# Modulation from float32 blocks, sums of weights on GpSimd, and a joined pair of tiles in the last product

## The chip, the cores and the metric

One core of a Trainium2 chip runs the whole kernel. The metric is the device time of one execution in microseconds (us). The engines are TensorE (PE, with its weight loads listed as PEld), VectorE (DVE), ScalarE (ACT), GpSimd (POOL) and SyncE (SP), which issues the DMA transfers.

## What is computed

Two layers act on 256 context tokens and 1024 latent tokens of width 1024; the last layer gives latent tokens only. A layer is:

```python
mod  = (silu(c)    @ ada_w + ada_b)      # 6 x 1024 values for latent tokens
modc = (silu(c_ctx) @ ada_w + ada_b)     # the same for context tokens
y  = mixer(x * (1 + sc1) + sh1, ...)     # input projection, two attentions, chunk gating, output projection
x  = layer_norm(ALPHA * x + g1 * y)
u  = dwconv3((x * (1 + sc2) + sh2) @ ffn_wup)
gate, val = split(u)
x  = layer_norm(ALPHA * x + g2 * ((silu(gate) * val) @ ffn_wdown))
```

`ada_w` is 1024 x 6144 per layer and meets only two vectors, `silu(c)` and `silu(c_ctx)`. `ffn_wup` is 1024 x 5632 and `ffn_wdown` 2816 x 1024.

## The kernel before, in words

**Precision.** Large products run in float32r on pairs: an operand is split into `hi` (a cast, mostly ACT, line 460) and `lo` (the rest, a subtraction on DVE or POOL, line 457), and a product is three matmuls (`mm3`, line 449). Small products use float32 directly; the trace shows two weight loads and two matmuls for each float32 matmul of the program.

**Order.** `Sched` (line 129) places every task by a table of assumed durations. A task has a key, which is its number in the program plus an offset; the lowest key that is ready goes first. `MODKEY` (120) is the offset of the modulation pieces and of the sums. The result is a fixed instruction stream per engine; SP issues its DMAs in that order, and a DMA that must wait holds those behind it.

**Modulation.** `mod_piece` (line 683) makes 256 of the 6144 values: 1 MB of `ada_w` is loaded in two or four blocks and split into `hi` and `lo`; 16 matmuls have the 4 columns of `s4` (the two vectors, high and low) as weights and 256 columns of `ada_w` moving; ACT copies the 4 x 256 result out, and two float32 matmuls with `sel4` add high and low and turn it into columns. There are 48 pieces. Eight are made at the start in `first_hT` (line 778), between the first products of the projection. The other 40 are fillers of `attention` (line 1302): 24 in layer 0, 16 in layer 1.

**Stages.** `first_hT`, then `in_proj` (line 842: chunks z, dk, dv, dq, kv, q, each over up to 10 tiles of 128 tokens), `attention`, `out_tiles`, `ffn` (line 1784). In the trace layer 0 has them at 0 to 85, 85 to 290, 290 to 850, 850 to 1085 (output projection and the first blocks of the up projection), and the rest of the feed-forward part up to 1910 us; layer 1 has its projection at 1910 to 2060, attention to 2570, output projection and first blocks to 2790, and the rest to the end.

**Feed-forward part.** Both products use seven half-size products in place of eight, which need sums of quarter blocks of the weights. For the up projection (22 blocks `f`) `up_load` (line 1554) loads the four quarters of a block and `up_operand` (line 1570) adds them to S1 to S4 (line 1480) before the split. For the down projection the four sums lie in `db` in DRAM. `sums` (line 581) makes them during attention by DMAs of POOL's queue: a copy and an accumulating copy, 16 per layer, 1408 KB each. `down_src` (line 1712) reads them.

**The tail.** The last of the seven down products of layer 1 (`tail` in `ffn`) runs its four pairs of tiles one after another, each over the 11 blocks `p` of weights: 33 matmuls of 512 columns per pair. The operands of `p` are split just before. After each tile's product come its residual sum and its normalisation.

Of the kernel before, what the change touches and what calls it, by code (L numbers as in the profile page):

```python
# [10 lines left out]
F32 = mybir.dt.float32  # L11
F32R = mybir.dt.float32r
# [57 lines left out]
SUMROWS = 704  # L70
# [320 lines left out]
class Kern:  # L391
# [185 lines left out]
    def flat(self, x, c):  # L577

        return x.rearrange("n p c -> (n p) c")[c * SUMROWS:(c + 1) * SUMROWS]

    def sums(self, l):

        x = self.db[l]
        w = lambda a, b: (lambda: self.i["w_down"][l, a, b])
        out = []

        def make(n, c, a, b, r=()):
            key = ("db", l, n, c)
            put = lambda: self.flat(x[n], c)
            kw = dict(w=[key], key=MODKEY, late=40.0)  # L590
            out.append(lambda: self.s.add({"pool": 1.0}, lambda e: self.nc.gpsimd.dma_start(out=put(), in_=self.flat(a(), c), max_dma_last_dim=2048), (), **kw))
            out.append(lambda: self.s.add({"pool": 1.0}, lambda e: self.nc.gpsimd.dma_start(out=put(), in_=self.flat(b(), c), accum_op=ALU.add, max_dma_last_dim=2048), [*r, key], **kw))

        for c in range(NP * P // SUMROWS):
            at = lambda n: ("db", l, n, c)
            make(0, c, w(0, 0), w(0, 1))
            make(1, c, w(0, 1), w(1, 1))
            make(2, c, w(1, 1), lambda: x[0], [at(0)])
            make(3, c, w(1, 0), lambda: x[2], [at(2)])
        return out  # L600

    def begin_sums(self, n):

        for f in self.due[:n]:
            f()
        del self.due[:n]

    def sum_chunks(self, name, l, n, f):
        a, b = f * P * 512, (f + 1) * P * 512 - 1
        m = SUMROWS * 512  # L610
        return [(name, l, n, c) for c in range(a // m, b // m + 1)]
# [28 lines left out]
    def setup(self):  # L640
# [9 lines left out]
        self.s4 = c.tile([P, KD, 4], F32R, tag="s4", name="s4")  # L650
        self.task(act_t(16), lambda e: nc.scalar.activation(s, cc, AF.Silu), ["cT"], ["silu"])
        self.task(dve_t(16), lambda e: nc.vector.tensor_copy(self.s4[:, :, 0:2], s), ["silu"], ["s4a"])
# [1361 lines left out]
```

## Time and profile before

| what | value |
|---|---|
| median of 3 runs | 3407.99 us (3407.11 to 3412.31) |
| the profiled execution | 3411.25 us |
| its span, first to last instruction | 3409.5 us |
| PE busy | 3186.5 us (93%) |
| DVE busy | 2700.5 us (79%) |
| ACT busy | 1677.3 us (49%) |
| POOL busy | 1028.0 us (30%) |
| mean granted clock of PE | 0.967 |
| DMA | 395.40 MB, mean 116 GB/s |

The busy time of an engine is the union of its instructions' times. The granted clock is a share of 2.4 GHz; it is either 1 or 0.5 (1.2 GHz) in any one stretch. In a line of instruction groups, the first number behind the bar is the busy time of the group, the second the mean duration of one instruction (ns). Matmuls overlap, so the distance between two of them is shorter than the duration of one.

### The profile page before, as it was taken

Reading aid. Unit: us, or ns where it says so; the run is one execution under the profiler, and the core shown is the slowest. Engines: PE = TensorE matmul, PEld = TensorE weight load, DVE = VectorE, ACT = ScalarE, POOL = GpSimd, SP = SyncE. Lnnn points to the kernel's source line nnn. Section 1 sums busy time; section 2 is a strip of 40 time slices with the busy share of each in tenths; the row PEclk is TensorE's granted clock in tenths of the full one; section 3 lists DMA queues with packets and bytes.
Section 4 is the critical chain, followed back from the end, with each engine's and each line's share of the span. In section 5 each row is a group of like instructions: output and inputs, shape, how many; then the busy total and the mean of one; then the engine's idle time right before and its main releaser. Section 6 shows DMA issues by size and latency. Waiting matters only on the chain. (4 is left out here: it accounts for less than half of the span.)

```text
span 3409.5 us, 53373 instructions
## 1 busy us (share of the span) xinstructions
PE 3186.5 (93%) x18953; PEld 2785.7 (82%) x18953; DVE 2700.5 (79%) x6407; ACT 1677.3 (49%) x2944; POOL 1028.0 (30%) x631
## 2 busy tenths in 40 slices
PE   7999898998988999999999999989999889999997
PEld 5998887887987888887877898878889867877775
DVE  7567887999768787886687757988998788888687
ACT  5125665666244444544444325665662455545542
POOL 3002554543112111121133302554532232322143
PEclk9999998999999999999999999999999999999998
DMA  6214443442312223225663314353423122323672
GB/s 242 72 52 112 118 124 99 126 108 86 121 69 70 89 72 101 87 86 180 210 204 130 116 58 123 92 135 87 119 88 127 62 80 96 107 98 105 229 258 99
DMA packets 258548, 395.40 MB, mean 116 GB/s; under 512 B 63976, under 2 KB 115688, under 8 KB 258280
## 3 DMA queue, kind: packets, MB, share of 16 engines
q1 hardware_dynamic: 240872, 345.84, 31.4%
q0 software_dynamic: 17408, 46.14, 5.9%
q8 instruction: 149, 2.44, 0.3%
q14 instruction: 119, 0.97, 0.1%
HBM read 311.61 MB, written 126.42 MB: 128 GB/s over the span
## 5 line engine op out<-in xcount | busy, mean ns | idle before, releaser
L447 PE MATMUL t<-region 128*128 128x512 f32 (+4 forms) x15631 | 2853.0, 341 | 137.8 <-DVE region L457 55.0
L447 PEld LDWEIGHTS t<-region 128*128 128x128 f32 x15631 | 2442.1, 192 | 480.0 <-DVE region L457 69.2
L457 DVE TENSOR_TENSOR region<-region 128x512 fp32r<-128x512 f32 (+6 forms) x873 | 760.0, 893 | 176.2 <-ACT region L460 122.7
L460 ACT ACTIVATE region<-region 128x512 fp32r<-128x512 f32 (+4 forms) x944 | 593.9, 663 | 382.8 <-PE t L447 132.5
L460 ACT ACTIVATE region<-t 128x512 fp32r<-128x512 f32 (+4 forms) x948 | 462.1, 514 | 600.0 <-PE t L447 386.3
L457 POOL TENSOR_TENSOR region<-region 128x512 fp32r<-128x512 f32 (+7 forms) x283 | 392.3, 1398 | 1109.3 <-ACT region L460 714.8
L1480 POOL TENSOR_TENSOR region<-region 128x512 f32<-128x512 f32 (+3 forms) x132 | 248.6, 1889 | 823.6 <-DVE region L1667 518.5
L1188 ACT ACTIVATE region<-region,q 128x1280 f32<-128x1280 f32 (+1 forms) x216 | 273.5, 1267 | 175.7 <-DVE q L1187 169.7
L1183 DVE TENSOR_SCALAR_CACHE_REDUCE region<-t 128x512 f32<-128x512 f32 (+1 forms) x600 | 333.7, 584 | 21.3 <-PE t L447 19.1
L457 DVE TENSOR_TENSOR region<-t,region 128x512 fp32r<-128x512 f32 (+1 forms) x529 | 296.9, 595 | 52.8 <-ACT region L460 50.9
L1667 DVE SCALAR_TENSOR_TENSOR region<-region,conv 128x1023 f32<-128x1023 f32 x176 | 231.6, 1325 | 36.7 <-ACT region L1665 36.5
L1480 DVE TENSOR_TENSOR region<-region 128x512 f32<-128x512 f32 (+3 forms) x301 | 226.3, 770 | 2.5 <-DMA da<-region 1.4
L1252 PE MATMUL t<-ident,region 128*128 128x128 f32 x1312 | 184.8, 285 | 24.2 <-DVE region L1225 8.1
L1228 POOL TENSOR_TENSOR region<-region 128x1280 f32<-128x1280 f32 (+1 forms) x68 | 186.8, 2746 | 5.7
L1665 ACT ACTIVATE region<-region,conv 128x1024 f32<-128x1024 f32 x88 | 109.2, 1241 | 159.5 <-DVE region L1648 148.3
L1252 PEld LDWEIGHTS t<-ident,region 128*128 128x128 f32 x1312 | 154.9, 147 | 31.8 <-DVE region L1183 11.0
L1227 POOL TENSOR_SCALAR region<-region,q 128x1280 f32<-128x1280 f32 (+1 forms) x68 | 84.5, 1242 | 210.6 <-DVE q L1222 137.7
L447 PE MATMUL t<-region,s 128*4 128x256 f32 x768 | 119.1, 291 | 17.0 <-DVE region L457 9.2
L447 PEld LDWEIGHTS t<-region,s 128*4 128x4 f32 x768 | 64.6, 87 | 47.4 <-DVE region L457 12.5
L548 POOL TENSOR_TENSOR region<-region 128x1024 f32<-128x1024 f32 x26 | 73.7, 2847 | 95.9 <-DMA region<-n 67.7
L1008 DVE TENSOR_TENSOR region<-t,region 128x256 f32<-128x256 f32 x32 | 13.6, 424 | 107.4 <-PE t L447 107.4
L548 DVE TENSOR_TENSOR region<-region 128x1024 f32<-128x1024 f32 x34 | 62.3, 1841 | 18.2 <-DMA region<-n 17.7
(134 smaller groups left out, 1803.5 us busy)
## 6 DMA issues: line engine op xcount, KB each, us to landing
region<-in_wup SPq DMA_DIRECT2D x176, 256.0 KB, 3.0
region<-in_ada_w SPq DMA_DIRECT2D x160, 256.0 KB, 3.1
da<-region SPq DMA_DIRECT2D x154, 256.0 KB, 3.0
region<-da SPq DMA_DIRECT2D x154, 256.0 KB, 4.1
db<-in_w_down POOLq DMA_DIRECT2D x24, 1408.0 KB, 7.5
region<-db SPq DMA_DIRECT2D x88, 256.0 KB, 4.1
region<-in_w_down SPq DMA_DIRECT2D x66, 256.0 KB, 3.9
n<-region SPq DMA_DIRECT2D x26, 512.0 KB, 3.0
```

The lines of the kernel that those rows point to most:

```text
L447: self.nc.tensor.matmul(ps, a, b, start=start, stop=stop, skip_group_check=again)
L457: eng.tensor_tensor(out=out, in0=full, in1=hi.bitcast(F32), op=ALU.subtract)
L460: self.nc.scalar.activation(out, in_, AF.Copy, **kw)
L548: self.task(engs or pool_t(D), lambda e, row=row, op=op: self.vec[e].tensor_tensor(out=x[:, :D], in0=x[:, :D], in1=row.t, op=op), [x, row] ...
L1183: self.task(dve_t(b - a), lambda e: nc.vector.tensor_scalar(p[:, a:b], ps[:, :b - a], -scale, None, op0=ALU.mult, op1=ALU.min, accum_out=n ...
L1188: self.task(act_t(nk, 0.19), lambda e: nc.scalar.activation(p[:, :nk], p[:, :nk], AF.Exp, bias=m.t, scale=-1.0, accum_out=s.t), [p, m], [p ...
L1227: nc.gpsimd.tensor_scalar(p2[:, :nk], p2[:, :nk], cc.t, 0.0, op0=ALU.mult, op1=ALU.add)
L1228: nc.gpsimd.tensor_tensor(out=p1[:, :nk], in0=p1[:, :nk], in1=p2[:, :nk], op=ALU.add)
L1252: nc.tensor.transpose(ps[:, u, j * P:(j + 1) * P], B[key][j][:, (kt + u) * P:(kt + u + 1) * P], self.ident)
L1480: self.task(engs or either(n), lambda e: self.vec[e].tensor_tensor(out=o(), in0=a(), in1=b(), op=op), r, w, **kw)
L1665: self.task(act_t(n, 0.15), lambda e: nc.scalar.activation(t.t, u(0, n), AF.Identity, scale=c[:, 1:2], bias=c[:, 3:4]), r + ["conv"], [t])
L1667: self.task(dve_t(n - 1, extra=0.06), lambda e, d=d: nc.vector.scalar_tensor_tensor(t[:, 1 - d:n - d], u(d, n - 1 + d), c[:, 2 * d:2 * d + ...
```

## The change

1. `mod_piece` has no split, no `s4` and no `sel4`. The raw float32 block is the weight operand (128 x 128 at a time) and the two columns of `silu` move: 2 halves x 8 steps, 16 float32 matmuls of 2 columns per piece, which write the values as columns at once.
2. The sums of `w_down` are made in `in_proj`: per block `p` SP loads the four quarters (4 x 256 KB), POOL makes four additions of 128 x 512, SP stores four results to `db`. The same is done for the first six blocks of `wup` into a new DRAM tensor `ws`. 17 such groups per layer are hung on the tiles of all chunks but z. POOL's DMAs are gone. For blocks 0 to 5 the up projection loads S1 to S4 ready-made (7 or 8 loads per block in place of 4) and adds nothing.
3. In the tail the first two pairs of tiles share one pass over `p`.

```diff
+    def sums(self, name, l, m):
+        up = name == "ws"
+        out = (self.ws if up else self.db)[l]
+        src = self.i["wup" if up else "w_down"]
+        z = [self.L(F32, (P, 2, HALF)) for _ in range(2)]
...
+                self.dma(lambda j=j, h=h: z[j][:, h], lambda j=j, h=h: src[l, j, h, m], 4 * P * HALF, w=[(z[j], h)], key=MODKEY)
...
+        t = [self.M() for _ in range(4)]
...
+            self.task(pool_t(HALF), lambda e, n=n, a=a, b=b: self.vec[e].tensor_tensor(out=t[n].t, in0=q[a][0](), in1=q[b][0](), op=ALU.add), [q[a][1], q[b][1]], [t[n]], key=MODKEY)
+            self.dma(lambda n=n: out[n, m], lambda n=n: t[n].t, 4 * P * HALF, [t[n]], [(name, l, n, m)], key=MODKEY)
 def mod_piece(self, l, n, key=0, raws=None):
-            w = [self.weight(x, 512, self.M, k=2, key=key, acq=True) for x in src]
...
-                    self.mm(ps[:4, :256], a, hi, h + k == 0, False)
-                    self.mm(ps[:4, :256], a, lo, False, kk * h + k == KD - 1)
-            self.task(mm_t(2 * kk, 256), go, ["s4"] + w[h][1], [ps], key=key, acq=[m4] if h == 0 else ())
-        self.task(act_t(256), lambda e: self.copy(m4[:4], ps[:4, :256]), [ps], [m4], key=key)
...
+            raws = [self.load(self.mod_src(l, n, h)[:, a:a + 512], 512, self.M, key) for h in range(2) for a in (0, 512)]
+            for c in range(2):
+                for k in range(KD):
+                    o = k % kk * 256 + c * P
+                    self.mm(pm[:, c], raws[k // kk][:, o:o + P], self.silu[:, k], k == 0, k == KD - 1)
+        self.task({"pe": 1.8}, go, ["silu", *raws], [pm], key=key)
 def in_chunk(self, l, name, tabs):
-        for t in tiles:
+        for n, t in enumerate(tiles):
+            if name != "z" and n % 4 == 1 and self.pairs_due:
+                self.sums("db", l, self.pairs_due.pop(0))
+            if name != "z" and n % 4 == 3 and self.blocks_due:
+                self.sums("ws", l, self.blocks_due.pop(0))
 def up_operand(self, l, m):
-        if n[0] == "S":
+        if n[0] == "S" and f >= UP_MADE:
 def ffn(self, l):
-                if tail:
+                if tail and m != 1:
                     for p in range(NP):
-                        self.down_mm(banks[t], *held[p], col(t), p, first)
+                        for x, _ in pairs[:2] if m == 0 else [(t, u)]:
+                            self.down_mm(banks[x], *held[p], col(x), p, first)
```

The scratch for dynamic DMAs goes from 2048 to 1024, since POOL issues none now. How the instruction streams move is seen at three places. A row is a run of like instructions of one engine: line, operation, output and inputs, shape, count. Counts of PE are the program's matmuls; a float32 one is two on the chip.

PE at the very start, before. `s` and `sel` are the tables named above, and `region` is any buffer.

```order
L447 MATMUL t<-region,s_70 4x256 x24
L447 MATMUL t<-sel_71,region 128x2 x2
L447 MATMUL t<-region,s_70 4x256 x16
L447 MATMUL t<-sel_71,region 128x2 x2
L447 MATMUL t<-region,s_70 4x256 x16
L447 MATMUL t<-sel_71,region 128x2 x2
L447 MATMUL t<-region,s_70 4x256 x8
L447 MATMUL t<-sel_71,region 128x2 x2
L447 MATMUL t<-region 128x512 x36
```

PE at the very start, now:

```order
L447 MATMUL t<-silu,region 128x2 x64
L447 MATMUL t<-region 128x512 x36
L447 MATMUL t<-silu,region 128x2 x48
L447 MATMUL t<-region 128x512 x36
L447 MATMUL t<-silu,region 128x2 x16
L447 MATMUL t<-region 128x512 x96
```

Four pieces still stand ahead of the first projection products, but in one run, then three, then one.

PE where attention of layer 0 begins, before (line 1168 is a transpose of queries, line 985 one of the projection):

```order
L1168 MATMUL t<-identr,region 128x128 x12
L447 MATMUL t<-region,s_70 4x256 x20
L447 MATMUL t<-sel_71,region 128x2 x2
L985 MATMUL t<-ident,region 128x128 x6
L447 MATMUL t<-region,s_70 4x256 x16
L447 MATMUL t<-sel_71,region 128x2 x2
L447 MATMUL t<-region 128x512 x12
```

The same place now:

```order
L1142 MATMUL t<-identr,region 128x128 x8
L447 MATMUL t<-silu,region 128x2 x48
L959 MATMUL t<-ident,region 128x128 x6
L447 MATMUL t<-region 128x512 x12
L447 MATMUL t<-region 128x256 x24
L447 MATMUL t<-region,sumj 128x256
```

Three pieces stand together here. Of the other 21 of this layer each stands alone; in layer 1 the first two stand together and 14 alone.

POOL in the input projection of layer 0, before, from its last splits of weights on:

```order
L457 TENSOR_TENSOR region<-region 128x1280
L1017 TENSOR_TENSOR region<-region 128x256
L457 TENSOR_TENSOR region<-region 128x1152
L591 DMA db<-in_w_down 704x512
L457 TENSOR_TENSOR region<-region 128x2x2x32
```

POOL there now (line 591 is the addition of a sum):

```order
L591 TENSOR_TENSOR region<-region 128x512 x2
L903 TENSOR_TENSOR region<-region 128x256 x2
L591 TENSOR_TENSOR region<-region 128x512 x16
L457 TENSOR_TENSOR region<-region 128x768
L591 TENSOR_TENSOR region<-region 128x512 x44
L457 TENSOR_TENSOR region<-region 128x1152
L591 TENSOR_TENSOR region<-region 128x512 x3
```

The additions fill POOL's stream there, and on SP their loads and stores stand between the loads of the chunks' weights, the last of which (`w_in_q`) comes behind most of the stores.

## Rows read from the trace of the kernel before

**Rows 1.** The page, busy time of the engines over the span.

```profile
PE 3186.5 (93%) x18953; PEld 2785.7 (82%) x18953; DVE 2700.5 (79%) x6407; ACT 1677.3 (49%) x2944; POOL 1028.0 (30%) x631
```

**Rows 2.** Span and mean granted clock of the core.

```profile
core 0: 3409.5 us, clock 0.967
```

**Rows 3.** Busy time by stage; stretch, length, engines' busy us, clock, DMA share, GB/s.

```profile
0.00:85.00 85.00, 64.79 (x328) 48.07 (x328) 65.08 (x118) 50.27 (x67) 27.36 (x18) 0.94 0.69 243
85.00:290.00 205.00, 203.49 (x1449) 198.24 (x1449) 118.58 (x585) 49.71 (x128) 17.68 (x16) 0.97 0.27 79
290.00:850.00 560.00, 509.32 (x3554) 453.95 (x3554) 481.17 (x1441) 349.90 (x690) 261.58 (x173) 0.95 0.39 108
1085.00:1910.00 825.00, 806.10 (x3991) 677.18 (x3990) 640.69 (x995) 396.31 (x626) 188.08 (x114) 0.99 0.41 130
1910.00:2060.00 150.00, 149.87 (x1120) 147.50 (x1119) 84.29 (x395) 31.07 (x80) 16.86 (x14) 1.00 0.21 66
2060.00:2570.00 510.00, 471.40 (x3283) 421.19 (x3281) 456.35 (x1347) 315.99 (x599) 225.53 (x141) 0.97 0.41 110
2570.00:2790.00 220.00, 194.11 (x1275) 176.61 (x1276) 180.69 (x415) 90.64 (x140) 66.25 (x38) 0.94 0.26 86
```

**Rows 4.** Groups of PE by shape, 35.6 to 38.4 us: modulation's matmuls of 256 columns.

```profile
L447 PE MATMUL t<-region,s 128*4 128x256 f32 x24 | 2.9, 276 | 0.0
```

**Rows 5.** Timeline of PE, 38 to 39.5 us: float32 matmuls of two columns.

```profile
38.43 0.60 PE L447 MATMUL t<-sel,region 4*128 4x2 f32 x4
```

**Rows 6.** Groups of PE by shape, 98.3 to 99.95 us: float32, 64 columns, full clock.

```profile
L447 PE MATMUL t<-region 128*128 128x64 f32 x16 | 1.9, 271 | 0.0
```

**Rows 7.** Groups of PE by shape, 85.3 to 88.3 us: the same at half clock.

```profile
L447 PE MATMUL t<-region 128*128 128x64 f32 x15 | 3.4, 423 | 7.5 <-issue 7.5
```

**Rows 8.** Busy time of three short stretches, columns as in rows 3.

```profile
85.30:88.30 3.00, 3.00 (x15) 3.00 (x15) 3.00 (x20) 0.00 (x0) 0.00 (x0) 0.50 0.00 0
286.30:289.70 3.40, 2.30 (x17) 1.52 (x14) 1.91 (x9) 2.56 (x8) 0.00 (x0) 1.00 0.99 299
289.70:293.10 3.40, 2.90 (x15) 1.57 (x15) 3.34 (x7) 1.96 (x4) 0.00 (x0) 0.50 0.73 256
```

**Rows 9.** Groups by shape, attention of layer 0 (290 to 850 us): splits of 512-column blocks.

```profile
L457 POOL TENSOR_TENSOR region<-region 128x512 fp32r<-128x512 f32 x62 | 82.7, 1345 | 142.1 <-ACT region L460 127.5 <-PE t L1252 7.4 <-DVE q L1220 5.2
L460 ACT ACTIVATE region<-region 128x512 fp32r<-128x512 f32 x94 | 56.6, 628 | 0.2
L457 DVE TENSOR_TENSOR region<-region 128x512 fp32r<-128x512 f32 x32 | 28.6, 901 | 0.4 <-ACT region L460 0.3
```

**Rows 10.** The same in attention of layer 1 (2060 to 2570 us).

```profile
L457 POOL TENSOR_TENSOR region<-region 128x512 fp32r<-128x512 f32 x39 | 52.1, 1343 | 80.4 <-ACT region L460 80.4
L460 ACT ACTIVATE region<-region 128x512 fp32r<-128x512 f32 x66 | 39.6, 627 | 2.4 <-DMA region<-in_ada_w 2.2
L457 DVE TENSOR_TENSOR region<-region 128x512 fp32r<-128x512 f32 x26 | 34.7, 1337 | 0.0
```

**Rows 11.** Groups by shape, whole span: float32 sums of 128 x 512.

```profile
L1480 DVE TENSOR_TENSOR region<-region 128x512 f32<-128x512 f32 x246 | 208.0, 848 | 1.8 <-DMA da<-region 1.4
L1480 POOL TENSOR_TENSOR region<-region 128x512 f32<-128x512 f32 x77 | 125.4, 1631 | 181.6 <-ACT region L1505 78.5 <-issue 25.5 <-DVE region L1764 19.2
```

**Rows 12.** Busy time, 28 to 33 us, columns as in rows 3.

```profile
28.00:33.00 5.00, 5.00 (x19) 3.97 (x18) 3.92 (x5) 2.06 (x2) 0.00 (x0) 0.77 1.02 405
```

**Rows 13.** Timeline of the tail, 3296 to 3410 us; start, length, engine, in brackets idle before.

```profile
3342.42 21.42 POOL L548 TENSOR_TENSOR region<-region 128x1024 f32<-128x1024 f32 x8 [4.23 <-ACT region L544]
3346.36 18.03 DVE L457 TENSOR_TENSOR region<-region 128x512 fp32r<-128x512 f32 x7 [4.68 <-ACT region L460]
3364.44 5.35 PE L447 MATMUL t<-region 128*128 128x512 f32 x14 [1.97 <-DVE region L457]
3372.29 23.34 PE L447 MATMUL t<-region 128*128 128x512 f32 x95 [2.50 <-DVE region L457]
```

More of the change, by code (lines that the diff above doesn't have):

```diff
@@ L69 @@
 UNIT = 64
-SUMROWS = 704
+UP_MADE = 6
 SLACK = 150
@@ L574, in row_from_col @@
         return row
[L577 to L600, printed above, removed]
@@ L649, in setup @@
         s = c.tile([P, KD, 2], F32, tag="silu", name="silu")
[L650 removed]
+        self.silu = s
         self.task(act_t(16), lambda e: nc.scalar.activation(s, cc, AF.Silu), ["cT"], ["silu"])
[L652 to L654 removed]
         self.modv, self.lnv, self.adab, self.inw = [], [], [], {}
@@ L676, in setup @@
         self.dc = d.tile([7, P, NP, P], F32, tag="dc", name="dc")
+        self.ws = [d.tile([4, UP_MADE, P, HALF], F32, tag=f"ws{l}", name="ws") for l in range(DEPTH)]
         self.db = [d.tile([4, NP, P, HALF], F32, tag=f"db{l}", name="db") for l in range(DEPTH)]
@@ L686, in mod_piece, with go @@
         j, q = QUADS[n // 4], n % 4
[L687 to L709 removed]
+        if not raws:
+            raws = [self.load(self.mod_src(l, n, h)[:, a:a + 512], 512, self.M, key) for h in range(2) for a in (0, 512)]
+        kk = KD // len(raws)
+        pm = self.bank(F32, (P, 2, 2))
+        def go(e):
+            for c in range(2):
[3 more added lines that the diff above has]
+        self.task({"pe": 1.8}, go, ["silu", *raws], [pm], key=key)
         ks = slice(2 * q, 2 * q + 2)
@@ L843, in in_proj @@
         tabs = self.tabs if l == 0 else self.z_tables(l)
+        self.pairs_due, self.blocks_due = list(range(NP)), list(range(UP_MADE))
         for name in ZCH:
@@ L1558, in up_load @@
             self.up_loaded += 1
-            for g, h in {"11": [(0, 0)], "12": [(0, 1)], "S1": [(1, 0), (1, 1)]}.get(n, ()):
+            if f < UP_MADE:
+                todo = [n]
+            else:
+                todo = {"S1": ["21", "22"]}.get(n, [n] if n in ("11", "12") else [])
+            for x in todo:
+                if x[0] == "S":
+                    j = int(x[1]) - 1
+                    src, r = self.ws[l][j, f], [("ws", l, j, f)]
+                else:
+                    src, r = self.i["wup"][l, int(x[0]) - 1, int(x[1]) - 1, f], []
                 raw = self.S(F32, (P, HALF))
-                self.dma(lambda raw=raw: raw.t, lambda f=f, g=g, h=h: self.i["wup"][l, g, h, f], 4 * P * HALF, (), [raw])
-                self.up_raw[f, g, h] = raw
+                self.dma(lambda raw=raw: raw.t, lambda src=src: src, 4 * P * HALF, r, [raw])
+                self.up_raw[f, x] = raw
     def up_operands(self, l, m):
@@ L1902, in program @@
             ada = [lambda a=a: self.mod_piece(*a, MODKEY) for a in ada]
-            self.due = self.sums(l)
-            m, d = len(ada), len(self.due)
-            fill = []
-            for j, a in enumerate(ada):
-                fill += [lambda: self.begin_sums(1)] * ((j + 1) * d // m - j * d // m) + [a]
-            self.attention(l, fill)
+            self.attention(l, ada)
             self.out_tiles(l, NT, True)
@@ L1997, in _arrays @@
     a["sel64"] = np.tile(np.eye(64, dtype=np.float32), (2, 1))
-    a["sel4"] = np.tile(np.eye(2, dtype=np.float32), (2, 1))
     return {k: np.ascontiguousarray(v) for k, v in a.items()}
```

41 lines of the change are left out of this document (11 added, 30 removed).

## The prediction

> **What bounds the kernel now.** I read the busy times over the span first. PE is busy 93% of it and DVE 79% [rows 1], so PE is the engine to price; its mean granted clock of 0.967 [rows 2] says that (1 - 0.967) x 2 x 3409.5 = 225 us ran at half clock, which cost some 112 us. Next come the busy times by stage [rows 3]. The input projections (85 to 290 and 1910 to 2060 us) and the long up and down products (1085 to 1910) leave PE idle for 1.5, 0.1 and 19 us: what is taken from DVE there gains little. The attentions are different: PE idles 560.0 - 509.3 = 51 us in layer 0 and 510.0 - 471.4 = 39 us in layer 1, while DVE is busy 86% and 89%. The starts of the up products are like them (layer 1: 2570 to 2790, PE idle 26 us, DVE busy 82%). So a change that moves work from DVE to PE must be read in attention, where 90 us of idle can be won and each us added to PE beyond that is lost.
>
> **The sum's base.** Durations are those of the profiled execution: 3411.25 us, of which 3409.5 are span and 1.75 lie around it. It stands 3.3 us above the median of the runs, 3407.99.
>
> **Modulation, PE's own work.** Before, a piece was 16 matmuls of 256 columns, which follow each other at (2.9 - 0.28)/23 = 0.114 us [rows 4], and four of the float32 matmuls with two columns, at (0.60 - 0.25)/3 = 0.117 us with a duration of 0.25 us [rows 5]: 1.82 + 0.47 = 2.3 us. Now it is 32 float32 matmuls on the chip, each with a 128 x 128 weight load and two columns. No row has this shape exactly. The bounds are two: the two-column matmuls with a weight of 128 columns but 4 rows, 0.117 us [rows 5], and those with a full 128 x 128 weight but 64 columns, (1.9 - 0.27)/15 = 0.109 us [rows 6]. Both say that the moving columns do not set the pace, since 2 and 64 cost the same; the weight load does. I take 0.112: 32 x 0.112 = 3.6 us at full clock. At half clock the 64-column ones follow at (3.4 - 0.42)/14 = 0.213 us [rows 7], so a piece takes 32 x 0.213 = 6.8 us. The 40 pieces in attention thus cost PE 40 x (3.6 - 2.3) = **+52 us** (bounds 48 and 58, by the two prices).
>
> **Modulation, the clock.** From 85.3 to 88.3 us PE was busy 3.00 of 3.00 us with float32 matmuls of 64 columns and their weight loads, and the granted clock was 0.50 throughout [rows 8]; unbroken work of that sort did not bring the clock up. And it fell after a stretch in which PE was busy 2.30 of 3.40 us (286.3 to 289.7) and then stayed at 0.50 for the next 3.4 us [rows 8], which costs 1.7 us of work. A piece has 2 columns per load where those had 64, and nothing else runs on PE while it lasts. I take it that three of four of the 35 pieces that stand alone lose 1.7 us each: 35 x 0.75 x 1.7 = 45. Three pieces together in layer 0 are 96 matmuls; I let a third of them run before the fall and 64 at 0.1 us more each, and 1.7 us is lost behind them: 8. Of the 64 of two pieces in layer 1 I let half run before it: 5. Together **+58 us**, with 0 and 130 (every one twice) as ends. The Trainium skill (TensorE: Matmul & The Clock Gate, section Why this matters for your kernels) asks only that no idle gaps stand between matmul bursts on PE; a piece leaves none, so by that rule this term would be 0 and the forecast 58 us lower. The row at 85.3 us differs from it: busy throughout, at half clock. Whether a weight load counts, the page does not say.
>
> **Modulation, what is relieved.** In attention the subtractions of the split blocks go: DVE loses 28.6 + 34.7 = 63 us, POOL 82.7 + 52.1 = 135 us and ACT 56.6 + 39.6 = 96 us (a few of them belong to other weights) [rows 9, 10]. DVE falls from 938 to 875 of 1070 us. PE's 90 us of idle come from several engines being late by little, and with PE slower too they shrink further: I take **-55 us**, between 0 (the idle lies in chains that do not change) and -80. POOL's DMAs leave as well; I cost that at nothing, DMA being busy 39% and 41% there [rows 3].
>
> **Modulation, the start.** The first 33 us are set by DMA (405 GB/s and a full share of 1.02 [rows 12]), and PE had only 64.8 of 85 us busy [rows 3]. PE starts cold. Now four pieces in a row run at half clock, 4 x 6.8 = 27; then three, a third of them at full clock, 3.6 + 13.6 = 17; then one, 4 to 5: 49 us against 8 x 2.3 = 18. That is +30, +3 for two more returns from half clock, less what of 20 us of idle can take it up: 6.5 at the very start cannot, some 6 between pieces can, and of the 7.5 us that PE waits at 85 us [rows 7] DVE's relief may win 4. With the half clock that the old first pieces had (2.5): **+20 us**, ends +5 and +35.
>
> **Sums on POOL in the projection.** 17 groups of four additions per layer at 1.63 us [rows 11] are 111 us of POOL, which was busy 18 of 205 and 17 of 150 us there [rows 3]: it fits, hidden behind PE. They bring 17 x 2 MB = 36 MB, or 174 and 238 GB/s on top of 79 and 66 [rows 3]; 405 was reached [rows 12]. SP's stores wait for POOL, and behind them wait the chunk weights; these are loaded two blocks ahead (IN_AHEAD), and a chunk lasts about 205/5 = 41 us. If that cover went, the last chunk, q, would start late. **+4 us**, ends 0 and +30. DVE gets slower beside a busy POOL, but has 86 us to spare of 205.
>
> **Ready-made S1 to S4.** 4 x 6 additions per layer leave DVE at 0.85 us [rows 11], 20 us each. Only those near the start of the up product, where PE idles, matter (12 in layer 1 and 8 in layer 0, 17 us of DVE). The extra loads (up to 4 x 256 KB per block) are hidden: 130 GB/s are moved there [rows 3] and 405 can be [rows 12]. **-8 us**, ends 0 and -20.
>
> **The tail.** POOL's 21.4 us of additions hold DVE's subtractions to 18.0/7 = 2.6 us each, and PE is starved from 3353 to 3372 us; then 95 matmuls remain [rows 13]. With two pairs per pass the second pair's 33 matmuls (33 x 23.34/95 = 8 us [rows 13]) fit into that starved time, except those of the last blocks. **-5 us**, ends 0 and -8. The end of the kernel is the last tile's normalisation, which moves with PE.
>
> **Sum.** 52 + 58 - 55 + 20 + 4 - 8 - 5 = +66: 3477 us against the profiled execution, **3474 us** against the median.
>
> **Rivals.** *The clock holds.* If weight loads keep the full clock, the 58 go, and so do about 15 of the start (its seven later records at half clock); the rest is -7, 3401 us. For it: PE is busy without gaps in a piece, all that the rule above asks. Against it: 85.3 us [rows 8]. Range 3385 to 3425.
> *DVE was the bound in attention.* Then the 63 us of DVE and the 135 of POOL decide, not PE: attention loses most of its 90 us of idle and, with fewer stalls, part of the 56 us that it had at half clock in layer 0 and 31 in layer 1 (5% and 3% short of full clock, doubled [rows 3]). That is -80 for the idle and -25 for the clock, against +52, and with the clock's loss around pieces at a quarter of mine (15): -38 instead of +55 in attention; the sum is -27, **3381 us**, faster. It decides from the point where DVE's relief exceeds what PE gains in work, 52 + 15 us. For it: DVE at 89%. Against: PE is busier, at 91 to 92%, and stays.
> *The projection stalls.* POOL's additions, slowed by DVE's work as DVE is by POOL's in the tail [rows 13], take 2.6 us each: 68 x 2.6 = 177 us, longer than layer 1's whole projection (150). SP's stores wait, the weights behind them come late, and PE idles by the difference, 27 us, there and as much in layer 0, where the last weights stand behind most of the stores: 3474 - 4 + 54 = 3524 us.
> That the change fails to relieve DVE is excluded: the splits are gone from the instruction stream.
>
> **Numbers.** The forecast gets 0.60, the clock that holds 0.14, DVE as the bound 0.14, the stall 0.12. 0.2% is about 7 us, what a measurement of this kernel can tell from no change. The forecast's own range, with attention's and the start's ends combined, is 3425 to 3520, and nearly all of it is slower. Of the clock case a third is faster, a third the same, a third slower; the DVE case is faster, the stall slower. Faster 0.17, same 0.06, slower 0.77. The range from 3390 to 3540 leaves out the lower part of the DVE case and the ends of the others.
>
> **What would show it.** In the new profile: two-column matmuls some 0.11 us apart at clock 1 and 0.21 at 0.5; the mean granted clock of both attentions below 0.95 and 0.97, with falls right behind pieces; PE busy more and DVE less there; both attentions longer; the first 85 us stage ending near 105; POOL at about 110 us of the projections and PE still full there; fewer idle us in the tail. The forecast is wrong if the clock stays up through the pieces, or if PE's idle time in attention falls by more than PE's work grows.

## The result and the profile after

The changed kernel takes **3521.37 us** in the median of 4 runs (3499.86 to 3527.49). The kernel before, timed beside it, takes 3409.84 us (3407.11 to 3412.31). The ratio is 1.0316, with a 95% interval of 1.027 to 1.0362: slower. The forecast was 3474 us, in a range of 3390 to 3540. The profiled execution took 3517.12 us.

The page's busy times, which answer to [rows 1], and the core's span and clock, which answer to [rows 2]:

```profile
PE 3312.9 (94%) x19529; PEld 2955.8 (84%) x19529; DVE 2647.9 (75%) x6279; ACT 1567.0 (45%) x2726; POOL 1037.9 (30%) x632
```

```profile
core 0: 3515.3 us, clock 0.948
```

PE is busy 126 us longer, while every other engine but POOL has less to do. The clock fell from 0.967 to 0.948, so (1 - 0.948) x 2 x 3515 = 366 us ran at half clock, where it was 225 before. Both figures leave out the first pieces of the start, as shown below.

The busy times by stage, columns as in [rows 3]. The stretches are the start, the two halves of layer 0's projection, its attention, and layer 1's projection and attention:

```profile
0.00:95.00 95.00, 85.94 (x399) 78.50 (x400) 31.14 (x69) 26.52 (x37) 7.83 (x12) 0.89 0.61 209
95.00:235.00 140.00, 127.67 (x903) 121.36 (x903) 89.32 (x275) 14.99 (x26) 76.06 (x59) 0.93 0.76 259
235.00:327.00 92.00, 83.91 (x528) 83.11 (x526) 69.66 (x327) 31.39 (x88) 23.91 (x20) 0.96 0.42 138
327.00:913.00 586.00, 564.51 (x3858) 530.02 (x3856) 441.74 (x1374) 299.51 (x582) 176.39 (x105) 0.90 0.23 69
1985.00:2165.00 180.00, 164.71 (x1177) 162.11 (x1176) 119.77 (x427) 36.95 (x96) 82.36 (x64) 0.95 0.67 222
2165.00:2682.00 517.00, 492.68 (x3338) 456.50 (x3337) 401.64 (x1212) 268.18 (x494) 161.71 (x86) 0.91 0.20 60
```

Two things differ from before. The attentions run at clock 0.90 and 0.91 instead of 0.95 and 0.97. The projections, in which PE was full before (203.5 of 205 and 149.9 of 150 us [rows 3]), now leave it idle, and their clock is 0.93 to 0.96.

Where the 105.8 us of longer span arose is read from the starts of the same matmuls in both traces. The table has the length of each stage before, and how much longer (+) or shorter it is in each kernel. The experiments of the next section stand beside the changed kernel, so that each can be looked up here.

| stage | before | after | old pieces | old sums | tail only | wide | no additions | DVE adds | old pieces, DVE adds | wide, DVE adds | before, no sums | new pieces, no sums |
|---|---|---|---|---|---|---|---|---|---|---|---|---|
| start | 71.2 | 23.1 | 0.9 | 23.7 | -0.4 | 3.3 | 23.4 | 23.9 | -1.1 | 2.9 | -1.6 | 23.5 |
| projection, layer 0 | 211.4 | 20.9 | 9.9 | -3.7 | -0.1 | 19.7 | -6.4 | 6.4 | 2.2 | 8.3 | -0.4 | -3.9 |
| attention, layer 0 | 557.9 | 28.0 | -13.6 | 40.5 | -0.2 | -14.8 | 33.1 | 37.5 | -9.9 | -6.9 | -17.9 | 40.1 |
| up to layer 1 | 1015.8 | -12.0 | -4.4 | 19.9 | -0.2 | -9.2 | -8.2 | -4.1 | -6.4 | -6.7 | 3.3 | 2.9 |
| projection, layer 1 | 220.6 | 27.5 | 27.7 | -0.9 | 0.0 | 27.5 | 1.8 | 5.8 | 8.5 | 5.5 | -0.1 | 3.5 |
| attention, layer 1 | 483.5 | 34.4 | 0.6 | 34.1 | -1.5 | 1.6 | 28.6 | 22.0 | 9.4 | -2.3 | 7.5 | 26.1 |
| start of its up product | 242.5 | -9.4 | -8.6 | 1.8 | 3.9 | -6.0 | -7.1 | -8.0 | -7.4 | -8.0 | 2.7 | 0.4 |
| the rest | 606.5 | -6.8 | -1.0 | 5.1 | -1.2 | -4.7 | 4.0 | 6.1 | -10.0 | 6.3 | -4.2 | 6.5 |

In the changed kernel the start costs 23 us, the attentions 62 and the projections 48; the rest gives back 28.

The pieces themselves. Groups of PE by shape in two stretches at the beginning of attention of layer 0, first at full clock (328.5 to 332 us), then at half (334 to 340):

```profile
L447 PE MATMUL t<-silu,region 128*128 128x2 f32 x32 | 3.7, 251 | 0.0
...
L447 PE MATMUL t<-silu,region 128*128 128x2 f32 x30 | 6.5, 352 | 0.0
```

The pace is (3.7 - 0.25)/31 = 0.111 us at full clock and (6.5 - 0.35)/29 = 0.212 at half. A piece, 32 of them on the chip, is 3.6 or 6.8 us of PE. These stretches belong to the three pieces that stand together, 96 matmuls. Busy times over the later part of them:

```profile
333.70:347.40 13.70, 13.70 (x62) 13.31 (x62) 2.38 (x8) 1.66 (x4) 0.00 (x0) 0.50 0.37 91
```

PE has not a moment of idle time and yet works at half clock throughout; the clock had fallen while PE was busy with these matmuls.

The same holds of the pieces that stand alone. The trace has 23 falls of the clock in the attention of layer 0; 20 of them come while a piece runs or within 1.6 us after its last matmul has begun. Of the pieces' 768 matmuls there only 104 follow each other at 0.21 us, so most of what the clock costs falls on the work behind a piece.

The start, timeline of PE (start, length, then the run of instructions), and the busy times over it:

```profile
5.50 27.44 PE L447 MATMUL t<-silu,region 128*128 128x2 f32 x128 [5.50 <-DMA region<-in_ada_w]
...
5.50:33.00 27.50, 27.44 (x128) 27.36 (x128) 0.84 (x6) 2.89 (x3) 0.00 (x0) 1.00 0.78 284
```

Four pieces take 27.4 us, as the forecast had it (27): 0.214 us per matmul, the pace that goes with half clock above. The clock column gives 1.00 here; the trace has no record of the clock before 40 us, and the column takes that as full, so half clock is read from the pace alone.

The projection is the surprise. The waits of PE in layer 0's, 95 to 327 us (engine, line, whom it waited for, us, times, longest):

```profile
PE t L969 <- DVE q L495: 5.6, 1, 5.6
PE t L447 <- DVE region L903: 5.0, 4, 2.4
PE t L447 <- DVE q L497: 3.7, 1, 3.7
PE t L447 <- issue: 3.6, 2, 2.0
PE t L969 <- DVE region L457: 2.5, 1, 2.5
```

Of these 20.4 us 16.8 end with DVE and none with DMA. Lines 493 to 499 are a chain of one-column instructions of DVE which yields an inverse square root. The transposes of line 969 do not need its result, but columns that DVE splits behind it (line 457), since DVE's order is fixed. The timeline of DVE, POOL and PE beside two such chains:

```profile
249.05 1.33 DVE L497 SCALAR_TENSOR_TENSOR q<-q 128x1 f32<-128x1 f32 x1
249.07 7.56 POOL L591 TENSOR_TENSOR region<-region 128x512 f32<-128x512 f32 x6 [3.63 <-DMA ws<-region]
250.41 0.15 DVE L498 TENSOR_SCALAR q<-q 128x1 f32<-128x1 f32 x1
250.60 1.02 DVE L499 TENSOR_TENSOR q<-q 128x1 f32<-128x1 f32 x1
251.66 1.21 DVE L497 SCALAR_TENSOR_TENSOR q<-q 128x1 f32<-128x1 f32 x1
...
258.10 0.21 DVE L457 TENSOR_TENSOR region<-region 128x64 fp32r<-128x64 f32 x1
258.37 0.37 PE L969 MATMUL t<-identr,region 128*128 128x128 f32 x1 [5.55 <-DVE q L495]
258.41 0.22 DVE L497 SCALAR_TENSOR_TENSOR q<-q 128x1 f32<-128x1 f32 x1
258.67 0.15 DVE L498 TENSOR_SCALAR q<-q 128x1 f32<-128x1 f32 x1
258.86 0.16 DVE L499 TENSOR_TENSOR q<-q 128x1 f32<-128x1 f32 x1
```

While POOL adds (249.07 to 256.63 us), DVE's one-column instructions with two tensor operands take 1.0 to 1.3 us, about one POOL addition (7.56/6 = 1.26 us), and the one-operand TENSOR_SCALAR between them its usual 0.15. Once POOL is through, the same instructions take 0.22 and 0.16. A chain has six of the held kind, so it comes some 6 x 1 us late, and PE starves behind it for 5.55 us. Longer instructions with two operands are held too: the additions of line 903 (128 x 256) take 0.67 us on average in this projection, and 0.41 in the kernel before.

The Trainium skill (GPSIMD Engine Reference, section 1. Specifications) says that GpSimd's interfaces to SBUF are shared with VectorE and that DVE instructions with two SBUF inputs contend there. The trace agrees, in which kind is held and which is not. The size here is a whole POOL addition per instruction.

The kernel before had shown this already, in the wait of PE that [rows 7] end with. Its timeline from 74 us on (line 457 is POOL's split of weights):

```profile
73.07 6.52 POOL L457 TENSOR_TENSOR region<-region 128x768 fp32r<-128x768 f32 x3
74.93 2.92 DVE L497 SCALAR_TENSOR_TENSOR q<-q 128x1 f32<-128x1 f32 x1
77.77 0.14 DVE L498 TENSOR_SCALAR q<-q 128x1 f32<-128x1 f32 x1
77.95 1.66 DVE L499 TENSOR_TENSOR q<-q 128x1 f32<-128x1 f32 x1
...
85.23 12.06 PE L447 MATMUL t<-region 128*128 128x64 f32 x43 [7.48 <-issue]
```

One-column instructions of 2.92 and 1.66 us stand beside POOL's splits of 6.52/3 = 2.17 us each, and PE sits idle for 7.48 us just then.

Idle time is not all of it. The two projection stages of the table, before, then in the changed kernel (columns as in [rows 3]; none has a piece in it):

```profile
71.20:282.60 211.40, 203.92 (x1428) 198.63 (x1428) 127.74 (x594) 48.38 (x119) 28.95 (x21) 0.97 0.24 69
1856.30:2076.90 220.60, 213.75 (x1450) 203.26 (x1449) 144.99 (x627) 69.31 (x149) 40.38 (x36) 0.98 0.28 87
...
94.30:326.60 232.30, 211.88 (x1428) 204.69 (x1428) 159.68 (x600) 46.37 (x114) 100.67 (x79) 0.94 0.63 211
1916.30:2164.40 248.10, 222.92 (x1451) 210.19 (x1450) 183.48 (x634) 66.94 (x144) 117.16 (x94) 0.94 0.62 208
```

PE idles 20.4 and 25.2 us where it idled 7.5 and 6.9, 31 us more. The other 17 of the 48 us answer to the clock, 0.94 where it was 0.97 and 0.98 (an estimate from these rows gives 18).

### The profile page after: what moved, and what is told of

Read it like the earlier page. It is cut to its first block, busy times and chain, and to the rows that moved or that the text cites. A ratio compares the mean times of both kernels' runs of the same rounds, so it can differ in the third digit from the quotient of the medians.

```text
span 3515.3 us, 54631 instructions
## 1 busy us (share of the span) xinstructions
PE 3312.9 (94%) x19529; PEld 2955.8 (84%) x19529; DVE 2647.9 (75%) x6279; ACT 1567.0 (45%) x2726; POOL 1037.9 (30%) x632
## 5 line engine op out<-in xcount | busy, mean ns | idle before, releaser
L447 PE MATMUL t<-region 128*128 128x256 f32 (+4 forms) x15631 | 2874.2, 344 | 137.1 <-DVE region L457 59.0
L447 PEld LDWEIGHTS t<-region 128*128 128x128 f32 x15631 | 2473.0, 195 | 477.7 <-DVE region L457 67.8
L457 DVE TENSOR_TENSOR region<-region 128x512 fp32r<-128x512 f32 (+6 forms) x796 | 699.9, 903 | 189.5 <-ACT region L460 148.0
L460 ACT ACTIVATE region<-t 128x512 fp32r<-128x512 f32 (+3 forms) x906 | 449.7, 523 | 751.5 <-PE t L447 412.9
L460 ACT ACTIVATE region<-region 128x512 fp32r<-128x512 f32 (+4 forms) x768 | 481.9, 661 | 332.4 <-PE t L447 151.9
L457 POOL TENSOR_TENSOR region<-region 128x512 fp32r<-128x512 f32 (+7 forms) x184 | 252.6, 1382 | 871.8 <-ACT region L460 291.4
L447 PEld LDWEIGHTS t<-silu,region 128*128 128x128 f32 x1536 | 215.9, 228 | 6.5 <-issue 5.5
L447 PE MATMUL t<-silu,region 128*128 128x2 f32 x1536 | 215.3, 276 | 5.6 <-DMA region<-in_ada_w 5.5
L591 POOL TENSOR_TENSOR region<-region 128x512 f32<-128x512 f32 x136 | 178.7, 1331 | 104.8 <-DMA region<-in_w_down 43.7
L1454 DVE TENSOR_TENSOR region<-region 128x512 f32<-128x512 f32 (+3 forms) x255 | 179.6, 722 | 3.1 <-POOL region L1454 2.4
```

The lines of the kernel that those rows point to most:

```text
L447: self.nc.tensor.matmul(ps, a, b, start=start, stop=stop, skip_group_check=again)
L457: eng.tensor_tensor(out=out, in0=full, in1=hi.bitcast(F32), op=ALU.subtract)
L460: self.nc.scalar.activation(out, in_, AF.Copy, **kw)
L591: self.task(pool_t(HALF), lambda e, n=n, a=a, b=b: self.vec[e].tensor_tensor(out=t[n].t, in0=q[a][0](), in1=q[b][0](), op=ALU.add), [q[a][ ...
L1454: self.task(engs or either(n), lambda e: self.vec[e].tensor_tensor(out=o(), in0=a(), in1=b(), op=op), r, w, **kw)
```

## The experiments

The theory from the trace of the changed kernel was: (A) the pieces cost the start and the attentions their time, and by the clock more than by PE's work; (B) POOL's additions cost the projections theirs, through DVE. Rivals: the attentions suffer from work alone; the projections from SP's queue and the traffic of DMA; the tail or the leaving of POOL's DMAs plays a part. Where a time of the kernel before is not given, it is within 2.3 us of 3409.84, as timed beside each.

**Old pieces.** The changed kernel with `mod_piece`, `s4` and `sel4` of before.

```diff
-                    self.mm(pm[:, c], raws[k // kk][:, o:o + P], self.silu[:, k], k == 0, k == KD - 1)
+                    self.mm(ps[:4, :256], a, hi, h + k == 0, False)
+                    self.mm(ps[:4, :256], a, lo, False, kk * h + k == KD - 1)
```

> The changed kernel with the modulation pieces of before (split blocks, 256 moving columns); sums on POOL and the joined tail stay. The changed trace shows +23 us in the start and +62 us in the two attentions, +44 in the two projections, -24 in the rest. If the start and the attentions are the pieces' doing (32 weight loads each, and the clock falls around them), 85 us go: 3521 - 85 = 3436 us, and the two projections stay 44 us longer than before. If they are lengthened by something else of the change (sums, buffers, DMA), most of the 85 stay and the time is near 3510.

Measured: 3421.99 us (3417.21 to 3429.05), ratio 1.0031 [1.0021, 1.0041]. The pieces are worth 99 us of the 112. The start is back at +0.9, the attentions are at -13.6 and +0.6, and the clock at 0.965. Layer 1's projection keeps +27.7 and layer 0's +9.9: that part does not come from the pieces. Why layer 0's is 11 us shorter than in the changed kernel, though no piece stands in it, no run tells. The kernel was faster than expected because layer 0's attention gained 13.6.

**Old sums.** The kernel before with the new pieces and the joined tail; sums by POOL's DMAs, nothing ready-made for the up product.

```diff
-                    self.mm(ps[:4, :256], a, hi, h + k == 0, False)
-                    self.mm(ps[:4, :256], a, lo, False, kk * h + k == KD - 1)
...
+                    self.mm(pm[:, c], raws[k // kk][:, o:o + P], self.silu[:, k], k == 0, k == KD - 1)
...
+                        for x, _ in pairs[:2] if m == 0 else [(t, u)]:
+                            self.down_mm(banks[x], *held[p], col(x), p, first)
```

> The kernel of before with the new modulation pieces and the joined tail; the sums are made by POOL's DMAs in attention as before. If the sums on POOL are what lengthens the projections (+44) and give 19 us back in the up products, then 3410 + 85 - 5 = 3490 us, with both projections as long as before. If the projections are long for another reason (a start that comes later, the clock), they stay long and the time is 3520 or more. Attention also gets its POOL DMAs back: if these cost anything there, it is above 62 us longer than before.

Measured: 3528.08 us (3524.28 to 3531.87), ratio 1.0342 [1.0328, 1.0357]; a miss by 38 us. The projections are free (-3.7 and -0.9), as expected. But the attentions cost 40.5 and 34.1 and the feed-forward part of layer 0 a further 19.9.

**Tail only.** The kernel before with the joined tail.

```diff
-                        self.down_mm(banks[t], *held[p], col(t), p, first)
+                        for x, _ in pairs[:2] if m == 0 else [(t, u)]:
+                            self.down_mm(banks[x], *held[p], col(x), p, first)
```

> The kernel of before with the joined tail alone. The changed trace gains 13 us up to the last 100 matmuls and loses 9 again behind them, 4.5 in all: 3410 - 5 = 3405 us. If the end is set by the normalisation of the tiles on DVE and not by PE, there is no change, 3410.

Measured: 3410.51 us (3404.31 to 3413.88), ratio 0.9996 [0.9987, 1.0005]: no change that can be measured. In the trace the stretch from 132 matmuls before the end to the last is 2.7 us shorter, which other stages take back.

**Wide.** The changed kernel with the same float32 weight loads, but 128 columns moving, the two of `silu` 64 times over; the first two are read. Work, order and sums are the same.

```diff
-        pm = self.bank(F32, (P, 2, 2))
+        pm = self.bank(F32, (P, 2, 64, 2))
...
-                    self.mm(pm[:, c], raws[k // kk][:, o:o + P], self.silu[:, k], k == 0, k == KD - 1)
+                    self.mm(pm[:, c], raws[k // kk][:, o:o + P], self.silu[:, k].unsqueeze(1).to_broadcast([P, 64, 2]), k == 0, k == KD - 1)
```

> The changed kernel with 128 moving columns in each matmul of a piece (the two columns repeated 64 times, 126 of the 128 results unused). If the pace is set by the weight load, a piece stays at 3.6 us at full clock; if the clock falls because next to nothing streams through PE, it now stays up: the mean granted clock returns from 0.948 to 0.965 or more, and of the 147 us more at half clock half come back, 73 us: 3450 us. If weight loads alone count for the clock or the falls come from elsewhere, clock and time stay (0.948, 3521), or the time grows by the columns (128 x 2 passes: up to 40 us).

Measured: 3429.66 us (3428.31 to 3432.04), ratio 1.0055 [1.0041, 1.0068]: 92 us less than the changed kernel, where 73 were expected. The core; its attentions by window (columns as in [rows 3]); and the pieces at the start in the timeline of PE:

```profile
core 0: 3426.8 us, clock 0.973
```

```profile
305.00:849.00 544.00, 519.57 (x3863) 484.07 (x3861) 444.08 (x1373) 297.88 (x582) 176.66 (x105) 0.99 0.25 74
2103.00:2589.00 486.00, 460.56 (x3348) 425.61 (x3346) 405.61 (x1215) 269.00 (x496) 161.74 (x86) 0.98 0.22 65
```

```profile
5.76 16.36 PE L447 MATMUL t<-silu,region 128*128 128x128 f32 x128 [5.76 <-DMA region<-in_ada_w]
```

The attentions hold as many matmuls as in the changed kernel (3863 and 3858, 3348 and 3338), run at 0.99 and 0.98, and are 42.8 and 32.8 us shorter. The first four pieces take 16.4 us for 27.4. An unbroken run of these matmuls at the beginning of attention, in the timeline of PE, gives (8.65 - 0.27)/75 = 0.112 us each, as with two columns at full clock:

```profile
309.73 8.65 PE L447 MATMUL t<-silu,region 128*128 128x128 f32 x76
```

PE's instructions stand in the same order in the attention of layer 0 as in the changed kernel, and PE idles as long (24.4 us for 21.5, 25.4 for 24.3). Of the 23 falls of the clock 3 are left there, none within 17 us behind a piece. So neither PE's work nor the weight loads add these 76 us to the attentions of the changed kernel, but the clock: 0.90 and 0.91 with two columns moving, 0.99 and 0.98 with 128. The projections, in which no piece stands, keep their +19.7 and +27.5.

**No additions.** The changed kernel without POOL's 136 additions. Every load and store stays.

```diff
-            self.task(pool_t(HALF), lambda e, n=n, a=a, b=b: self.vec[e].tensor_tensor(out=t[n].t, in0=q[a][0](), in1=q[b][0](), op=ALU.add), [q[a][1], q[b][1]], [t[n]], key=MODKEY)
-            self.dma(lambda n=n: out[n, m], lambda n=n: t[n].t, 4 * P * HALF, [t[n]], [(name, l, n, m)], key=MODKEY)
+            x = b if a[0] == "t" else a
+            self.dma(lambda n=n: out[n, m], q[x][0], 4 * P * HALF, [q[x][1]], [(name, l, n, m)], key=MODKEY)
```

> The changed kernel without POOL's 136 additions: the quarters are loaded and one of the two operands of each sum is stored in its place (the sums are left out; loads and stores stay). The projections are 44 us longer in the changed kernel, 10 of it between the first kv and the first q tile of layer 0 and 19 between first kv and last q of layer 1. If POOL's additions hold DVE's short chains, these 10 and 19 go to 1 or less and DVE's one-column operations fall from 0.28 and 0.36 us to 0.17 and 0.26: 3521 - 37 = 3484 us. If SP's queue or the DMA traffic of the sums makes them late, both stay: 3521 us.

Measured: 3480.37 us (3476.33 to 3489.34), ratio 1.0202 [1.0178, 1.0226]. The projections go from +20.9 and +27.5 to -6.4 and +1.8: with all 36 MB per layer still moving and as many DMAs in SP's queue, nothing stalls. That excludes the traffic. It does not exclude weights that come late behind stores that wait for POOL, since no store waits for an addition here. The changed kernel's own trace does: no instruction in it waits for a load of the weights of dk, dv, dq, kv or q, and the last load for q in layer 0 is issued at 252.0 us, 30 us ahead of q's first product. DVE's chain in the stage of the kv chunk (groups by shape), in the changed kernel (235 to 284 us), then without additions (216 to 256):

```profile
L497 DVE SCALAR_TENSOR_TENSOR q<-q 128x1 f32<-128x1 f32 x27 | 9.5, 352 | 0.7
L499 DVE TENSOR_TENSOR q<-q 128x1 f32<-128x1 f32 x27 | 8.7, 322 | 0.6
L498 DVE TENSOR_SCALAR q<-q 128x1 f32<-128x1 f32 x27 | 4.1, 152 | 0.7
```

```profile
L497 DVE SCALAR_TENSOR_TENSOR q<-q 128x1 f32<-128x1 f32 x27 | 7.6, 280 | 0.9
L499 DVE TENSOR_TENSOR q<-q 128x1 f32<-128x1 f32 x26 | 4.1, 158 | 0.7
```

The means hide it: seldom is a chain held, but then for 6 us in a row. Even here one instruction of line 497 takes 1.87 us, beside a split of POOL of 1.85 us. Of the 53 us that go in the projections, 41 arrive at the end; the feed-forward parts gain less.

**DVE adds.** The changed kernel with the additions on DVE.

```diff
-            self.task(pool_t(HALF), lambda e, n=n, a=a, b=b: self.vec[e].tensor_tensor(out=t[n].t, in0=q[a][0](), in1=q[b][0](), op=ALU.add), [q[a][1], q[b][1]], [t[n]], key=MODKEY)
+            self.task(dve_t(HALF), lambda e, n=n, a=a, b=b: self.vec[e].tensor_tensor(out=t[n].t, in0=q[a][0](), in1=q[b][0](), op=ALU.add), [q[a][1], q[b][1]], [t[n]], key=MODKEY)
```

> The changed kernel with the additions on DVE in place of POOL. DVE gets 68 x 0.68 = 46 us per layer in projections where it was busy 119 of 205 and 84 of 150 us. If what hurts is that POOL holds DVE's operations, most of the 44 us go (a DVE addition of 0.68 us ahead of a chain costs that once, not at each of its steps): 3490 us. If any 1 MB group of sums in the projection delays the chains by its sheer work or traffic, the time stays at 3521 or grows.

Measured: 3506.53 us (3500.91 to 3517.39), ratio 1.0278 [1.0254, 1.0301]. The projections fall to +6.4 and +5.8, though DVE, the engine PE waits for there, has more to do. The sums on DVE, 224 to 268 us:

```profile
L591 DVE TENSOR_TENSOR region<-region 128x512 f32<-128x512 f32 x19 | 13.0, 682 | 0.0
```

0.68 us each where POOL needs 1.33. Line 497 is no faster on average in this stretch than in the changed kernel (0.363 us), but what holds it now is a few long splits of POOL, not a row of additions:

```profile
248.52 2.66 POOL L457 TENSOR_TENSOR region<-region 128x1152 fp32r<-128x1152 f32 x1 [27.89 <-DVE q L497]
248.53 2.67 DVE L497 SCALAR_TENSOR_TENSOR q<-q 128x1 f32<-128x1 f32 x1
```

The hold has the length of POOL's instruction again. Only 15 us arrive at the end. The projections are 36 us shorter than in the changed kernel and layer 1's attention 12; but layer 0's attention is 9.5 us longer, and its feed-forward part and the rest of layer 1 gain 21 less. Why, no run tells.

**Old pieces, DVE adds.** The two repairs together: the edit of "old pieces" and that of "DVE adds" on the changed kernel.

```diff
-                    self.mm(pm[:, c], raws[k // kk][:, o:o + P], self.silu[:, k], k == 0, k == KD - 1)
+                    self.mm(ps[:4, :256], a, hi, h + k == 0, False)
+                    self.mm(ps[:4, :256], a, lo, False, kk * h + k == KD - 1)
...
+            self.task(dve_t(HALF), lambda e, n=n, a=a, b=b: self.vec[e].tensor_tensor(out=t[n].t, in0=q[a][0](), in1=q[b][0](), op=ALU.add), [q[a][1], q[b][1]], [t[n]], key=MODKEY)
```

> Old modulation pieces, sums on DVE in the projection, ready-made S1 to S4 for six blocks, joined tail. The run with the old pieces and sums on POOL took 3422 with some 38 us lost in the projections. If DVE's additions cost 5 to 10 of these instead, 3392 us, below both kernels. If the delay is in the sums' traffic, 3422.

Measured: 3390.71 us (3386.12 to 3396.5), ratio **0.9935 [0.9917, 0.9954]**: faster than both kernels, and within 1 us of what was expected. Clock 0.967, as before the change.

**Wide, DVE adds.** The changed kernel with both the wide columns and the additions on DVE.

```diff
+                    self.mm(pm[:, c], raws[k // kk][:, o:o + P], self.silu[:, k].unsqueeze(1).to_broadcast([P, 64, 2]), k == 0, k == KD - 1)
...
+            self.task(dve_t(HALF), lambda e, n=n, a=a, b=b: self.vec[e].tensor_tensor(out=t[n].t, in0=q[a][0](), in1=q[b][0](), op=ALU.add), [q[a][1], q[b][1]], [t[n]], key=MODKEY)
```

> 128 moving columns in the pieces and the sums on DVE. From 3430 with POOL's additions, with some 42 us lost in the projections: if DVE's additions cost 5 to 10 of these, 3395 us, and the attentions stay 13 us shorter than before in all. If the delay is in the sums' traffic, 3430.

Measured: 3413.97 us (3410.36 to 3416.12), ratio 1.0004 [0.9994, 1.0013]: no change against the kernel before, and 19 us above what was expected. Both its attentions are shorter than before (-6.9 and -2.3). Against the same kernel with the old pieces it loses 4 us at the start, 6 in layer 0's projection and 16 in the rest; the last of these isn't explained.

**Before, no sums.** The kernel before without POOL's 32 DMAs, to see what their leaving is worth; the down product reads plain quarter blocks.

```diff
-            self.due = self.sums(l)
+            self.due = []
-            return (lambda: self.db[l][self.DB[i], p]), self.sum_chunks("db", l, self.DB[i], p)
+            return (lambda: self.i["w_down"][l, j, h, p]), []
```

> The kernel before without POOL's 32 sum DMAs in the attentions; the four down products that used ready-made sums read plain quarter blocks of the weights instead (so their values are not the sums), everything else as before. Isolates what POOL's DMAs cost the attentions. My prediction costed them at nothing: by it the time is that of before, 3410, and attention of layer 0 stays at 558 us. Theory after the earlier runs: the DMAs cost layer 0's attention 13 us and layer 1's nothing; time 3397 (3390 to 3405), attention of layer 0 at 544 to 547. Rival: the 13 us came from the other order of the work that the filler list without sums gives; then also about 3397 here, but with the relief without fewer or faster waits; if the gain came from the ready-made sums in the up product, nothing changes here: 3410.

Measured: 3399.72 us (3392.04 to 3409.98), ratio 0.9967 [0.9955, 0.9978]. Layer 0's attention is 17.9 us shorter, layer 1's 7.5 longer. The first of these answers to the 13.6 that "old pieces" gained: without POOL's DMAs layer 0's attention is shorter. Whether the DMAs themselves had that price is not shown, since PE's instructions stand in another order there without them, and the rival of that order is left. The window of that attention in the kernel before and here:

```profile
283.00:840.00 557.00, 508.50 (x3563) 452.11 (x3562) 476.79 (x1411) 350.01 (x693) 259.48 (x171) 0.95 0.40 111
```

```profile
285.00:829.00 544.00, 502.43 (x3554) 448.82 (x3554) 487.00 (x1422) 349.47 (x693) 248.18 (x159) 0.97 0.26 77
```

The moved bytes fall from 111 to 77 GB/s, PE idles 41.6 us instead of 48.5, and the clock is 0.97 instead of 0.95. Which of these came first, the trace doesn't tell.

**New pieces, no sums.** The kernel of "old sums" with the same DMAs taken out.

> The kernel e2_old_sums (new modulation pieces, sums by POOL's DMAs, joined tail) with the same DMAs taken out and the plain quarter blocks read. e2 was 3528, with attentions at +40 and +34 us and an unexplained +20 us in the feed-forward part of layer 0. If the DMAs cost layer 0's attention 13 us beside the new pieces too, attention of layer 0 is at +28 and the time at about 3515 or, if the +20 us in the feed-forward part came from the DMAs too (sums that are late, or their traffic), 3495. Rival: the new pieces alone bring the +20 us there by another order of the work; then it stays, and the time is 3510 to 3528.

Measured: 3517.03 us (3510.23 to 3522.3), ratio 1.0314 [1.0297, 1.0331]. The 19.9 us in the feed-forward part fall to 2.9, so they came with the DMAs: by their traffic, by sums that came late, or by another order of the work. The attention of layer 0 stays at 40.1: beside the new pieces it gains nothing without the DMAs. The changed kernel has 28.0 there; what its other order of work gains, 12 us, stays open.

## Why the prediction was right

The sign, the range and the main mechanism held; the forecast was 47 us too low. One term alone was 44 us too low; what the others missed nearly cancels, and that they cancel is luck.

- **PE's work of a piece**: 0.112 us per matmul forecast, 0.111 measured at full clock; 0.213 and 0.212 at half. That the two columns do not set the pace held as well: 128 cost 0.112.
- **The clock**, +58 forecast: the mechanism is shown by the wide columns, and the size by them is 42.8 + 32.8 = 76 us in the attentions. The place where it falls was forecast too: behind pieces that stand alone and within those that stand together. The row that the forecast set against the clock that holds was a weak one: the same matmuls of 64 columns ran on without a gap, and the clock came back to 1.00 at 95 us with nothing else on PE. The rule of the Trainium skill cited there (TensorE: Matmul & The Clock Gate, section Why this matters for your kernels: no idle gaps between bursts) would have given 0. Here it does not suffice: from 333.7 to 347.4 us PE had no gap and the clock was at 0.50.
- **Work less relief**: 52 - 55 = -3 forecast. The wide kernel, with the clock up, has attentions of together -13.2 us, and the old pieces with the same sums -13.0. So the two forms are equal there, as the forecast had it, but not for its reason. PE's idle time in the attentions is 83 us before, 70 with the old pieces and the new sums, and 50 in the wide kernel: the splits that go relieve PE by 20 us, not 55. The rest of the balance is the clock, 0.99 and 0.98 in the wide kernel for 0.96 with the old pieces, some 26 us by these figures (an estimate). That the term came out near -3 is luck.
- **The attentions together**: +55 forecast, +62 measured, which is some +75 against the old pieces with the same sums, less the 13 that those gain.
- **The start**: +20 forecast, +23 measured; four pieces at the pace of half clock took 27.4 us for 27.
- **Sums on POOL in the projection**: +4 (0 to 30) forecast, +48 measured, 53 by what the run without additions takes away. This is the step that failed. It asked whether POOL has time for the additions and whether SP's queue brings weights late, and dismissed DVE with "DVE gets slower beside a busy POOL, but has 86 us to spare of 205". Spare time was the wrong measure: PE waits for results behind a chain of DVE with six short instructions of two operands, and beside POOL's additions each of them waits for one whole addition. The falls of the clock that follow were not in the term either. The rival of the stalled projection had the place and nearly the size (54), but another mechanism, weights that come late in SP's queue, and in the changed kernel's trace nothing waits for those.
- **POOL's DMAs that leave the attentions**, costed at nothing: the kernel before is 18 us shorter without them in layer 0's attention and 7.5 longer in layer 1's, 11 us shorter in all, by the DMAs or by the other order of the work. A mean DMA share of 40% did not show it.
- **Ready-made S1 to S4**, -8: the start of the up product in layer 1 is 6 to 9 us shorter wherever they are used, and layer 0 up to layer 1 is 4 to 12 shorter in the same kernels. That is some 15 together, of which half was forecast; no run has them alone.
- **The tail**, -5: -2.7 in the trace alone, nothing in the time.

The rivals: the clock that holds fell by the changed kernel and came true in the wide one, at 3430 instead of 3401, mainly because the projections cost 47 us there and not 4. DVE as the bound of the attentions fell: in the wide kernel DVE was relieved and the clock up, and the attentions gained 13 us together, not the 80 + 25 - 52 = 53 that the rival had, and no more than with the old pieces.

## What to carry to other kernels

When work is moved to a free engine, look for short dependent chains on other engines that will run beside it and that PE waits for; free time on either engine says nothing about them. Price a product against two vectors, with the matrix as weights, at half clock too: here it ran there without a pause on PE, 128 moving columns at the same weight loads kept the clock up, and the old form with the matrix moving was 8 us faster over the kernel than that, and 23 with the sums on DVE. Of a change with several parts, run the parts apart: old pieces and the sums moved to DVE gave 0.9935, while the whole change gave 1.0316.

## What was not expected of the hardware

- With float32 weight loads and two columns per matmul, PE ran at half clock without an idle moment (13.70 of 13.70 us busy at 0.50). With 128 columns per load the mean clock was 0.973, higher than in the kernel before (0.967).
- The pace of these loads is the same for 2, 64 and 128 columns: 0.111, 0.109 and 0.112 us at full clock.
- One-column DVE instructions with two tensor operands took 1.0 to 1.3 us beside POOL's additions of 1.26, 2.67 beside a split of 2.66, and 0.16 to 0.22 without; those with one tensor operand took 0.15 in both.
- The same 128 x 512 additions took 0.68 us on DVE and 1.33 on POOL in the projections.
- Without the 16 DMAs of POOL's queue layer 0's attention was 18 us shorter in the kernel before, at a mean DMA share of 0.40, and beside the new pieces no shorter (40.5 and 40.1). The cause is open.
